# Gates of a product-key expert layer: both parts summed in PSUM and multiplied into G by VectorE

## The chip, the cores and the metric

One core of a Trainium2 chip runs the kernel. The metric is the time of one execution in microseconds (us) on the device; the figure compared is the median of several runs. Engines are named as in the profile: PE is TensorE (PEld its weight loads), DVE is VectorE, ACT is ScalarE, POOL is GpSimd, SP is the queue that issues the transfers.

## The reference, cut to what matters

Two layers; each has a token mixer and then an expert layer (PEER). The expert layer works on 1024 real tokens (and 16 meta tokens in the first layer) with 4096 experts. Per token and head (8 heads), product keys choose 16 experts and a softmax gives each a gate:

```
g = softmax(best_s).reshape(t, 128)                  # 8 heads x 16 gates per token
h_all = einsum('td,nd->tn', xt, u)                   # every expert's hidden value
a = gelu(take_along_axis(h_all, idx)) * g
w = zeros((t, 4096)).at[arange(t)[:, None], idx].add(a)
out = w @ v
```

The kernel computes it densely: G holds, for every expert and token, gelu(hidden) times the sum of the gates that chose this expert (zero for most), and out is G times v.

## The kernel before, in words

The tokens of a layer are worked through in two halves: P (528 tokens in the first layer, with the meta tokens, 512 in the second) and Q (512). An expert's index is m * 32 + r, with m (0 to 127) on the partitions and r a row of 0 to 31, so G is a tile of 128 x 32 x 528 in f32.

- `route` (DVE) finds the 16 experts of each head and token; `slots` turns the result round with PE transposes, so that the 128 choices of a token lie on the partitions: `P.mT` (m of each choice), `P.rT` (its r) and the gate times 2^15 in a high and a low f16 part, `P.gh` and `P.gl`.
- `hidden` loops over the rows r: 24 products (in the first layer's P 48, since its two spans of 272 and 256 tokens are apart) make one row of hidden values in PSUM (L1104), and ACT writes gelu of it into G (L1113). Tokens whose gates are there already take another way: ACT writes gelu into a temporary `ga` (L1110) and POOL multiplies it into G (L1111). In P each piece of weights is split first: ACT rounds it (L273), POOL takes the difference (L280), and SP stores it. In Q the difference is read back instead.
- `gates`, called from `hidden` between rows, does 16 tokens at a time. DVE builds a one-hot matrix `Lh` of m (L1142, 128 x 2048, f16), a one-hot `R[0]` of r (L1144), and the products of `R[0]` with the high part (L1146) and the low part (L1147), each 128 x 512. PE multiplies, for each of the 16 tokens, `Lh` (128 choices x 128 m) by the two parts (128 choices x 32 r).
- In P (L1171) the two parts are 32 products into the same 32 columns of one PSUM bank, so that PSUM adds them. In Q (`P.wide`, L1159) they are 16 products of 64 columns into two banks; ACT copies the high part (L1164) and DVE adds the low part (L1165).
- For the rows that `hidden` has not reached, ACT writes the gates into G (in P L1175), where L1111 meets them later. For the n rows that it has passed, the gates go through ACT (and in Q DVE) into a temporary `gt`, and POOL multiplies them into G: `POOL.tensor_tensor(G[:, 0:n, t0:t0 + 16], gt[:, 0:n], G[:, 0:n, t0:t0 + 16], op=ALU.mult)` (L1177).
- In P the gates are spread over rows 17 to 29 (33 calls in the first layer and 32 in the second, some 2.7 to a row); in Q over rows 6 to 31 (32 calls in each layer, 1.3 to a row). `values` (L1203, L1204, L1209) then multiplies G by v; its first row needs all gates.

`Lh` and `R` have two buffers each, the ring "g" of PSUM has banks 2 and 3 (2 to 5 in Q's gates), and `gt` shares three buffers "ht" with `ga` and with loads. The program is written in the order of the code; a planner, which simulates the engines when the kernel is built, sets the order of instructions on each engine's queue from what it expects to be ready. Each engine then works through its queue in order.

Of the kernel before, what the change touches and what calls it, by code (L numbers as in the profile page):

```python
# [12 lines left out]
F32 = mybir.dt.float32  # L13
# [15 lines left out]
MM = ((3, 0, 2, 0, 0, 3, 0, 0), (3, 0, 2, 0, 0, 3, 0, 0))  # L29
PEND = 29  # L30
QE = 31
WIDE = True
D = 1024
KT = 8
META = 16
# [27 lines left out]
def tile_trunk(ctx, tc, h0, w_pk, wgate, w2, glab, w_out, wqT, keysT, u_pk, v_w, sinks,  # L63
# [30 lines left out]
    for t in ("ah", "al"):  # L94
# [2 lines left out]
    g0 = lay(1, [("wraw", 512, 4), ("ht", 528, 3), ("nsq", 528, 1), ("ndg", 128, 2), ("acc", T, 1), ("nms", 8, 2),  # L97
                 ("nrs", 8, 2), ("rb", 272, 2), ("kt", 128, 2)], 0)
    o = lay(1, [("G", G_EL, 1), ("s", 4096, 1), ("mS", 320, 1), ("rS", 320, 1), ("gS", 640, 1), ("mT", 264, 1), ("rT", 264, 1),
                ("gh", 264, 1), ("glo", 264, 1)], g0)  # L100
    end_p = max(lay(1, [("L", 1024, 2), ("R", 768, 2)], o),
                lay(1, [("X", 1280, 1), ("V", 320, 3), ("I", 320, 3), ("C", 640, 1), ("W", 160, 1), ("J", 160, 1),
                        ("qi", 160, 1), ("rmx", 10, 1), ("rsr", 10, 1)] + [(f"rt{i}", 80, 1) for i in range(8)], o))
    end_p = lay(1, [("iotaM", 256, 1), ("iotaR", 64, 1), ("startT", 80, 1), ("pidxT", 80, 1)], end_p)
# [830 lines left out]
    def peer_setup(qa, qb):  # L935

        P = Layer()
        P.sp = sp = Span(qa.c0, qb.c1)
        P.parts = [(0, qa), (qa.w, qb)]
        P.merge = qa.w == qb.w  # L940
        P.mS = sb([128, 5, 128], F16, "mS")
        P.rS = sb([128, 5, 128], F16, "rS")
        P.gS = sb([128, 5, 128], F32, "gS")
        P.s = [None] * 4
        P.ns = 4 if len(sp.tiles) == 4 else 3
        P.mT = sb([128, 528], F16, "mT")
        P.rT = sb([128, 528], F16, "rT")
        P.gh = sb([128, 528], F16, "gh")
        P.gl = sb([128, 528], F16, "glo")
        P.rows = P.gated = 0  # L950
        P.wide = False
        return P

    def yv(half, lo, k, o, w):
# [163 lines left out]
    def slots(P):  # L1118

        sp = P.sp  # L1120
        for j, (o, m) in enumerate(sp.tiles):
            tp = ps1("g").bitcast(F16)[:, 0:256].rearrange("p (a b) -> p a b", a=2)
            PE.transpose(tp[:, 0, 0:m], P.mS[0:m, j, :], ident16[0:m, 0:m])
            PE.transpose(tp[:, 1, 0:m], P.rS[0:m, j, :], ident16[0:m, 0:m])
            DVE.tensor_copy(P.mT[:, o:o + m], tp[:, 0, 0:m])
            DVE.tensor_copy(P.rT[:, o:o + m], tp[:, 1, 0:m])
            tg = ps1("g")
            PE.transpose(tg[:, 0:m], P.gS[0:m, j, :], ident[0:m, 0:m])
            ACT.activation(P.gh[:, o:o + m], tg[:, 0:m], AF.Copy, scale=GSC)
            DVE.scalar_tensor_tensor(P.gl[:, o:o + m], tg[:, 0:m], GSC, P.gh[:, o:o + m], op0=ALU.mult,  # L1130
                                     op1=ALU.subtract)

    def gates(P, G, iotaM, iotaR):

# [3 lines left out]
        def v4(a, n):  # L1138
# [1 line left out]

        Lh = sb([128, 4, 128, 4], F16, "L", 2)
        DVE.tensor_tensor(Lh, iotaM.unsqueeze(1).to_broadcast([128, 4, 128, 4]), v4(P.mT, 128), op=ALU.is_equal)  # L1142
        R = sb([128, 3, 4, 32, 4], F16, "R", 2)
        DVE.tensor_tensor(R[:, 0], iotaR.unsqueeze(1).to_broadcast([128, 4, 32, 4]), v4(P.rT, 32),  # L1144
                          op=ALU.is_equal)
        DVE.tensor_tensor(R[:, 1], R[:, 0], v4(P.gh, 32), op=ALU.mult)  # L1146
        DVE.tensor_tensor(R[:, 2], R[:, 0], v4(P.gl, 32), op=ALU.mult)  # L1147
        n = P.rows
        gt = sb([128, 32, 16], F32, "ht") if n else None
        outs = [(G[:, n:32, t0:t0 + 16], n, 32)] if n < 32 else []  # L1150
        if n:
            outs.append((gt[:, 0:n], 0, n))
        if P.wide:

            for u in range(2):
                ps = ps1("g")
                for i in range(8 * u, 8 * u + 8):
                    b, t = i // 4, i % 4
                    PE.matmul(ps[:, i % 8 * 64:i % 8 * 64 + 64].rearrange("p (a r) -> p a r", a=2), Lh[:, b, :, t],  # L1159
                              R[:, 1:3, b, :, t], start=True, stop=True)  # L1160
                pv = ps.rearrange("p (t a r) -> p a r t", a=2, r=32)
                for dst, lo, hi in outs:
                    dv = dst[:, :, 8 * u:8 * u + 8]
                    ACT.activation(dv, pv[:, 0, lo:hi], AF.Copy, scale=1.0 / GSC)  # L1164
                    DVE.scalar_tensor_tensor(dv, pv[:, 1, lo:hi], 1.0 / GSC, dv, op0=ALU.mult, op1=ALU.add)  # L1165
        else:
            ps = ps1("g")
            for i in range(16):
                b, t = i // 4, i % 4
                for part in (1, 2):  # L1170
                    PE.matmul(ps[:, i * 32:(i + 1) * 32], Lh[:, b, :, t], R[:, part, b, :, t], start=(part == 1),  # L1171
                              stop=(part == 2))
            pv = ps.rearrange("p (t r) -> p r t", r=32)
            for dst, lo, hi in outs:
                ACT.activation(dst, pv[:, lo:hi], AF.Copy, scale=1.0 / GSC)  # L1175
        if n:
            POOL.tensor_tensor(G[:, 0:n, t0:t0 + 16], gt[:, 0:n], G[:, 0:n, t0:t0 + 16], op=ALU.mult)  # L1177
        P.gated = t0 + 16

    def values(*args, **kw):  # L1180
# [79 lines left out]
    for l in range(DEPTH):  # L1260
# [177 lines left out]
```

## Time and profile before

| | |
|---|---|
| median of 3 runs | 3380.03 us (3378.39 to 3394.43) |
| the profiled execution | 3392.98 us, of which the span 3391.3 us |
| busy share of the span | PE 93%, PEld 78%, DVE 64%, ACT 41%, POOL 32% |
| mean granted TensorE clock | 0.955 of 2.4 GHz |

The span runs from the first to the last instruction of the profiled execution, and times inside it count from its start. That execution is 0.4% above the median of the runs. P's gates lie from about 921 to 1043 us (first layer) and from 2592 to 2724 us (second layer); Q's from about 1365 to 1545 us and from 3010 to 3185 us. A busy share says how long an engine had an instruction in hand, waits for a port included.

### The profile page before, as it was taken

How to read it: one execution, taken by the hardware profiler on the slowest of the kernel's cores; microseconds unless marked ns; L12 is line 12 of the kernel's file. 1: busy time of each engine (PE TensorE's matmuls, PEld its weight loads, DVE VectorE, ACT ScalarE, POOL GpSimd, SP SyncE). 2: the span in 40 equal slices, each digit the busy share in tenths (PEclk: the TensorE clock that was granted, in tenths of full speed). 3: DMA queues.
4: the chain of work that ended last, by engine and by line, in shares of the span. 5: the costliest groups of instructions: out<-in, count | busy, mean ns of one | idle time of the engine just before them, and what ended most of it. 6: DMA issues, size and time to landing. Idle time of an engine off the chain costs nothing.

```text
span 3391.3 us, 64331 instructions
## 1 busy us (share of the span) xinstructions
PE 3157.8 (93%) x22459; PEld 2647.5 (78%) x22459; DVE 2172.3 (64%) x7020; ACT 1381.1 (41%) x3278; POOL 1091.0 (32%) x1092
## 2 busy tenths in 40 slices
PE   7999999989788989999898999999898889999998
PEld 6686887679788988787775868876776678688788
DVE  4645446579896589663326454455698957976547
ACT  4534334433334434444344343344333344344355
POOL 4314022224475232131401231223245643313325
PEclk9899999989889999999997999999898899999999
DMA  8767774564324555445964687755753256554555
GB/s 284 236 202 247 257 245 146 174 217 164 125 88 158 182 178 189 163 152 191 331 232 151 210 274 241 232 170 167 251 173 125 94 179 221 183 189 151 180 173 156
DMA packets 397222, 651.27 MB, mean 192 GB/s; under 512 B 43536, under 2 KB 109152, under 8 KB 396896
## 3 DMA queue, kind: packets, MB, share of 16 engines
q1 hardware_dynamic: 396896, 647.16, 59.3%
q8 instruction: 176, 2.88, 0.4%
q14 instruction: 150, 1.23, 0.1%
HBM read 489.56 MB, written 157.42 MB: 191 GB/s over the span
## 4 chain that ended last, share of the span: by engine, by line
PE 59%; DVE 23%; DMA 6%; ACT 2%; issue 2%; POOL 1%; SPq 0%; POOLq 0%; DVEq 0%; ACTq 0%
PE b L1209 14%; PE b L1104 13%; PE b L334 12%; PE b L980 4%; DVE arena L1142 2%; DMA arena<-h 2%; PE b L704 2%; DVE arena_r L1204 2%; PE b L1159 2%; DVE arena L998 2%; DVE arena L999 2%; PE b L758 1%; DVE arena L1001 1%; PE b L619 1%; DVE arena L1147 1%
## 5 line engine op out<-in xcount | busy, mean ns | idle before, releaser
L280 POOL TENSOR_TENSOR arena_r<-arena,arena_r 128x512 fp32r<-128x512 f32 (+1 forms) x453 | 561.0, 1246 | 867.9 <-ACT arena_r L273 813.9
L1104 PE MATMUL b<-arena_r 128*128 128x512 f32 (+2 forms) x3840 | 782.3, 363 | 23.4 <-ACT arena L1113 13.5
L1209 PE MATMUL b<-arena_r 128*128 128x512 f32 (+2 forms) x4224 | 755.4, 337 | 36.5 <-DVE arena_r L1204 24.7
L1209 PEld LDWEIGHTS b<-arena_r 128*128 128x128 f32 x4224 | 643.8, 190 | 135.8 <-DVE arena_r L1204 41.9
L1104 PEld LDWEIGHTS b<-arena_r 128*128 128x128 f32 x3840 | 643.5, 197 | 123.4 <-ACT arena L1113 14.1
L334 PE MATMUL b<-arena_r 128*128 128x256 f32 (+1 forms) x4992 | 694.6, 293 | 33.8 <-ACT arena_r L273 10.2
L334 PEld LDWEIGHTS b<-arena_r 128*128 128x128 f32 x4992 | 635.1, 193 | 74.4 <-issue 21.8
L273 ACT ACTIVATE arena_r<-arena 128x512 fp32r<-128x512 f32 x456 | 285.1, 629 | 472.4 <-PE b L1104 124.4
L1204 DVE TENSOR_TENSOR arena_r<-arena,arena_r 128x512 fp32r<-128x512 f32 (+2 forms) x352 | 260.5, 751 | 230.9 <-ACT arena_r L1203 230.1
L307 ACT ACTIVATE arena_r<-arena 128x512 fp32r<-128x512 f32 x284 | 178.5, 631 | 327.4 <-PE b L1209 130.5
L980 PE MATMUL b<-arena_r 128*128 128x256 f32 (+1 forms) x1632 | 220.6, 291 | 15.3 <-DMA arena_r<-m_0l 5.3
L1142 DVE TENSOR_TENSOR arena<-arena 128x2048 f16<-128x2048 f16 x129 | 178.8, 1388 | 83.8 <-PE b L1159 83.7
L980 PEld LDWEIGHTS b<-arena_r 128*128 128x128 f32 (+1 forms) x1632 | 205.4, 190 | 27.9 <-DMA arena_r<-m_0l 7.3
L1177 POOL TENSOR_TENSOR arena<-arena 128x448 f32<-128x448 f32 (+20 forms) x129 | 144.2, 1123 | 150.8 <-DVE arena L1165 115.4
L1203 ACT ACTIVATE arena_r<-arena 128x512 fp32r<-128x512 f32 (+2 forms) x352 | 171.7, 502 | 25.2 <-PE b L1209 23.6
L256 POOL TENSOR_TENSOR arena<-arena 128x256 f32<-128x256 f32 (+2 forms) x105 | 90.7, 864 | 271.4 <-ACT arena L255 264.2
L280 DVE TENSOR_TENSOR arena_r<-arena,arena_r 128x256 fp32r<-128x256 f32 (+1 forms) x187 | 101.0, 546 | 92.1 <-ACT arena_r L273 71.2
L716 DVE TENSOR_TENSOR_SCAN arena<-arena,zf 128x384 f32<-128x384 f32 (+6 forms) x116 | 104.3, 903 | 79.0 <-ACT arena L711 77.8
L1111 POOL TENSOR_TENSOR arena<-arena 128x272 f32<-128x272 f32 (+25 forms) x86 | 95.1, 1110 | 158.4 <-DVE arena L1165 141.0
L422 ACT ACTIVATE arena<-b 128x256 f32<-128x256 f32 (+1 forms) x144 | 55.3, 384 | 202.0 <-PE b L334 201.2
L577 POOL TENSOR_TENSOR arena<-arena,mhalf 128x8 f32<-128x8 f32 (+3 forms) x43 | 63.6, 1479 | 210.5 <-DVE arena L574 143.3
L1171 PE MATMUL b<-arena 128*128 128x32 f16 x2080 | 83.5, 192 | 34.2 <-DVE arena L1142 15.9
(273 smaller groups left out, 4240.8 us busy)
## 6 DMA issues: line engine op xcount, KB each, us to landing
arena<-in_v_w_dram SPq DMA_DIRECT2D x288, 256.0 KB, 2.9
arena<-in_u_pk_dram SPq DMA_DIRECT2D x256, 256.0 KB, 3.0
arena_r<-a_0h SPq DMA_DIRECT2D x108, 256.0 KB, 3.7
arena_r<-a_0l SPq DMA_DIRECT2D x108, 256.0 KB, 4.0
arena_r<-a_1h SPq DMA_DIRECT2D x108, 256.0 KB, 3.3
arena_r<-a_1l SPq DMA_DIRECT2D x108, 256.0 KB, 3.9
arena<-m SPq DMA_DIRECT2D x92, 256.0 KB, 4.3
arena<-in_w_pk_dram SPq DMA_DIRECT2D x72, 256.0 KB, 4.3
```

The source lines that it names most:

```text
L273: ACT.activation(hi, src, AF.Copy)
L280: e.tensor_tensor(lo[:, a:b], src[:, a:b], hi[:, a:b].bitcast(F32), op=ALU.subtract)
L307: ACT.activation(hi, wload(src), AF.Copy)
L334: PE.matmul(ps, wt[:, ks], x.at(low, k, xo, sp.w), start=(k == 0 and i == 0), stop=(k == KT - 1 and i == 2))
L716: DVE.tensor_tensor_scan(keep[0:m, 0:wd][:, ::-1], keep[0:m, 0:wd][:, ::-1], zf[0:m, 0:1].to_broadcast([m, wd]), keep[0:m, wd:wd + 1], op0 ...
L980: PE.matmul(ps, yv(half, low, k, oo, m), wt[:, kk * 256:kk * 256 + 256], start=(k == 0 and i == 0 and e == 0), stop=(k == KT - 1 and i == ...
L1104: PE.matmul(ps, wt[:, ks], yv(h, low, k, 0, w // 2 if h is None else w), start=(k == 0 and i == 0), stop=(k == KT - 1 and i == 2))
L1142: DVE.tensor_tensor(Lh, iotaM.unsqueeze(1).to_broadcast([128, 4, 128, 4]), v4(P.mT, 128), op=ALU.is_equal)
L1177: POOL.tensor_tensor(G[:, 0:n, t0:t0 + 16], gt[:, 0:n], G[:, 0:n, t0:t0 + 16], op=ALU.mult)
L1203: ACT.activation(ah, G[:, r, o:o + w], AF.Copy)
L1204: last = DVE.tensor_tensor(al, G[:, r, o:o + w], ah.bitcast(F32), op=ALU.subtract)
L1209: PE.matmul(ps, wt[:, d * 128:d * 128 + 128], pr[low], start=(opens and r == 0 and i == 0), stop=(closes and r == 31 and i == 2))
```

## The change

`gates` has one form for P and Q. The high and low gates lie beside each other in one tile `P.gg`, which `slots` fills; one DVE instruction multiplies `R0` (broadcast over the two parts) by both (128 x 1024). PE always makes 32 products of 32 columns, and PSUM adds the parts. DVE multiplies the n passed rows into G straight from PSUM with one `scalar_tensor_tensor`, in place of ACT's copy into `gt` and POOL's product. ACT still writes the other rows. The four-bank ring of Q's gates goes.

```diff
-        P.gh = sb([128, 528], F16, "gh")
-        P.gl = sb([128, 528], F16, "glo")
+        P.gg = sb([128, 132, 2, 4], F16, "gg")
...
-            ACT.activation(P.gh[:, o:o + m], tg[:, 0:m], AF.Copy, scale=GSC)
-            DVE.scalar_tensor_tensor(P.gl[:, o:o + m], tg[:, 0:m], GSC, P.gh[:, o:o + m], op0=ALU.mult,
-                                     op1=ALU.subtract)
+            g4 = tg[:, 0:m].rearrange("p (b t) -> p b t", t=4)
+            gh, gl = [P.gg[:, o // 4:(o + m) // 4, a] for a in range(2)]
+            ACT.activation(gh, g4, AF.Copy, scale=GSC)
+            DVE.scalar_tensor_tensor(gl, g4, GSC, gh, op0=ALU.mult, op1=ALU.subtract)
...
-        R = sb([128, 3, 4, 32, 4], F16, "R", 2)
-        DVE.tensor_tensor(R[:, 0], iotaR.unsqueeze(1).to_broadcast([128, 4, 32, 4]), v4(P.rT, 32),
-                          op=ALU.is_equal)
-        DVE.tensor_tensor(R[:, 1], R[:, 0], v4(P.gh, 32), op=ALU.mult)
-        DVE.tensor_tensor(R[:, 2], R[:, 0], v4(P.gl, 32), op=ALU.mult)
+        R0 = sb([128, 4, 32, 4], F16, "R0")
+        DVE.tensor_tensor(R0, iotaR.unsqueeze(1).to_broadcast([128, 4, 32, 4]), v4(P.rT, 32), op=ALU.is_equal)
+        R = sb([128, 4, 2, 32, 4], F16, "R")
+        DVE.tensor_tensor(R, R0.unsqueeze(2).to_broadcast([128, 4, 2, 32, 4]),
+                          P.gg[:, t0 // 4:t0 // 4 + 4].unsqueeze(3).to_broadcast([128, 4, 2, 32, 4]), op=ALU.mult)
         n = P.rows
...
+        ps = ps1("g")
+        for i in range(16):
+            b, t = i // 4, i % 4
+            for part in range(2):
+                PE.matmul(ps[:, i * 32:(i + 1) * 32], Lh[:, b, :, t], R[:, b, part, :, t], start=(part == 0),
+                          stop=(part == 1))
+        pv = ps.rearrange("p (t r) -> p r t", r=32)
         if n:
-            POOL.tensor_tensor(G[:, 0:n, t0:t0 + 16], gt[:, 0:n], G[:, 0:n, t0:t0 + 16], op=ALU.mult)
+            gv = G[:, 0:n, t0:t0 + 16]
+            DVE.scalar_tensor_tensor(gv, pv[:, 0:n], 1.0 / GSC, gv, op0=ALU.mult, op1=ALU.mult)
+        if n < 32:
+            ACT.activation(G[:, n:32, t0:t0 + 16], pv[:, n:32], AF.Copy, scale=1.0 / GSC)
...
-        Q.wide = WIDE
...
-        set_rings(g=(2, 3, 4, 5))
         hidden(l, Q, G, HQ, 32, "h", cst, QE)
-        set_rings(g=(2, 3))
```

## Rows read from the trace of the kernel before

**Rows 1.** Stretch, length, busy us (instructions) of PE, PEld, DVE, ACT, POOL; clock, DMA

```profile
921.00:1043.00 122.00, 105.26 (x1503) 102.05 (x1502) 116.70 (x124) 40.48 (x116) 92.00 (x68) 0.88 0.27 88
2592.00:2724.00 132.00, 111.12 (x1301) 91.60 (x1299) 117.49 (x118) 44.19 (x114) 94.79 (x69) 0.86 0.31 102
1365.00:1545.00 180.00, 177.06 (x1130) 144.44 (x1129) 108.37 (x266) 78.61 (x232) 55.43 (x60) 0.98 0.47 149
3010.00:3185.00 175.00, 171.04 (x1113) 140.35 (x1111) 108.14 (x267) 76.76 (x230) 58.19 (x59) 0.99 0.47 150
```

**Rows 2.** Chain of waits by line, 921 to 1043 us, then 2592 to 2724 us

```profile
by line: DVE arena L1142 34.2%; DVE arena L1147 21.3%; DVE arena L1146 13.7%; PE b L1104 9.2%; PE b L1171 7.6%; DVE arena L1144 6.8%; issue 6.3%; ACT arena L1175 0.5%; DVE arena_r L1204 0.4%; DVEq L1146 0.0%
...
by line: PE b L1104 35.1%; DVE arena L1142 20.1%; PE b L1171 13.6%; DVE arena L1147 12.3%; DVE arena L1146 7.5%; issue 5.1%; DVE arena L1144 3.9%; DMA arena<-h 1.5%; POOL arena L1111 1.0%; ACT arena L1175 0.2%
```

**Rows 3.** Groups by line, 921 to 1043 us: count | busy us, mean ns | idle before

```profile
L1142 DVE TENSOR_TENSOR arena<-arena 128x2048 f16<-128x2048 f16 x31 | 48.8, 1574 | 0.0
L1171 PE MATMUL b<-arena 128*128 128x32 f16 x1056 | 43.7, 191 | 16.7 <-DVE arena L1142 7.3 <-DVE arena L1147 5.9 <-DVE arena L1146 2.5
L1177 POOL TENSOR_TENSOR arena<-arena 128x288 f32<-128x288 f32 (+11 forms) x32 | 43.2, 1354 | 15.8 <-ACT arena L1175 15.8
...
L1147 DVE TENSOR_TENSOR arena<-arena 128x512 f16<-128x512 f16 x31 | 30.3, 979 | 0.0
L1146 DVE TENSOR_TENSOR arena<-arena 128x512 f16<-128x512 f16 x31 | 26.2, 846 | 5.8 <-PE b L1171 5.7
...
L1144 DVE TENSOR_TENSOR arena<-arena 128x512 f16<-128x512 f16 x29 | 17.8, 646 | 0.1
```

**Rows 4.** The same groups, 2592 to 2724 us

```profile
L1142 DVE TENSOR_TENSOR arena<-arena 128x2048 f16<-128x2048 f16 x30 | 46.9, 1563 | 0.0
L1177 POOL TENSOR_TENSOR arena<-arena 128x288 f32<-128x288 f32 (+11 forms) x32 | 43.0, 1349 | 18.3 <-ACT arena L1175 15.5 <-PE b L1104 2.3 <-DMA u_0l<-arena_r 0.5
L1171 PE MATMUL b<-arena 128*128 128x32 f16 x1024 | 39.7, 192 | 17.5 <-DVE arena L1142 8.6 <-DVE arena L1147 6.2 <-DVE arena L1146 2.5
...
L1147 DVE TENSOR_TENSOR arena<-arena 128x512 f16<-128x512 f16 x30 | 28.9, 965 | 0.0
L1146 DVE TENSOR_TENSOR arena<-arena 128x512 f16<-128x512 f16 x30 | 27.4, 914 | 12.6 <-PE b L1171 12.5
L1144 DVE TENSOR_TENSOR arena<-arena 128x512 f16<-128x512 f16 x28 | 21.8, 804 | 0.1
```

**Rows 5.** Lines L1142 and L1146 over the span: min/median/max ns

```profile
L1142 DVE TENSOR_TENSOR arena<-arena x129: 1207/1218/2332, 904.7 to 3172.4; 128x2048 f16<-128x2048 f16 x129
...
L1146 DVE TENSOR_TENSOR arena<-arena x129: 409/420/1524, 907.5 to 3173.5; 128x512 f16<-128x512 f16 x129
```

**Rows 6.** L1165 by shape over the span: count | busy us, mean ns

```profile
L1165 DVE SCALAR_TENSOR_TENSOR arena<-b,arena 128x64 f32<-128x64 f32 x12 | 2.3, 214 | 0.3 <-ACT arena L1164 0.3
...
L1165 DVE SCALAR_TENSOR_TENSOR arena<-b,arena 128x248 f32<-128x248 f32 x4 | 1.5, 408 | 0.0
```

**Rows 7.** Timeline, 1455 to 1459 us, POOL then DVE: start, duration

```profile
1455.55 1.69 POOL L1111 TENSOR_TENSOR arena<-arena 128x272 f32<-128x272 f32 x1 [4.58 <-DVE arena L1165]
...
1456.52 0.25 DVE L1165 SCALAR_TENSOR_TENSOR arena<-b,arena 128x96 f32<-128x96 f32 x1
1456.68 0.83 DVE L1146 TENSOR_TENSOR arena<-arena 128x512 f16<-128x512 f16 x1
```

**Rows 8.** Timeline of PE: two gates in Q, then two in P

```profile
1440.90 2.17 PE L1159 MATMUL b<-arena 128*128 128x64 f16 x32
...
2592.56 2.32 PE L1171 MATMUL b<-arena 128*128 128x32 f16 x64
```

**Rows 9.** Chain of waits behind Q's last gate, 1528 to 1540 us: start, us

```profile
1530.62 0.45 ACT arena L1164 x2
...
1531.16 0.85 DVE arena L1165 x3
...
1532.08 2.41 POOL arena L1177 x2
```

More of the change, by code (lines that the diff above doesn't have):

```diff
@@ L31 @@
 QE = 31
-WIDE = True
 D = 1024
@@ L99, in tile_trunk @@
     o = lay(1, [("G", G_EL, 1), ("s", 4096, 1), ("mS", 320, 1), ("rS", 320, 1), ("gS", 640, 1), ("mT", 264, 1), ("rT", 264, 1),
-                ("gh", 264, 1), ("glo", 264, 1)], g0)
-    end_p = max(lay(1, [("L", 1024, 2), ("R", 768, 2)], o),
+                ("gg", 528, 1)], g0)
+    end_p = max(lay(1, [("L", 1024, 2), ("R0", 256, 2), ("R", 512, 2)], o),
                 lay(1, [("X", 1280, 1), ("V", 320, 3), ("I", 320, 3), ("C", 640, 1), ("W", 160, 1), ("J", 160, 1),
@@ L947, in peer_setup @@
         P.rT = sb([128, 528], F16, "rT")
-        P.gh = sb([128, 528], F16, "gh")
-        P.gl = sb([128, 528], F16, "glo")
+        P.gg = sb([128, 132, 2, 4], F16, "gg")
         P.rows = P.gated = 0
-        P.wide = False
         return P
@@ L1142, in gates @@
         DVE.tensor_tensor(Lh, iotaM.unsqueeze(1).to_broadcast([128, 4, 128, 4]), v4(P.mT, 128), op=ALU.is_equal)
-        R = sb([128, 3, 4, 32, 4], F16, "R", 2)
-        DVE.tensor_tensor(R[:, 0], iotaR.unsqueeze(1).to_broadcast([128, 4, 32, 4]), v4(P.rT, 32),
-                          op=ALU.is_equal)
-        DVE.tensor_tensor(R[:, 1], R[:, 0], v4(P.gh, 32), op=ALU.mult)
-        DVE.tensor_tensor(R[:, 2], R[:, 0], v4(P.gl, 32), op=ALU.mult)
-        n = P.rows
-        gt = sb([128, 32, 16], F32, "ht") if n else None
@@ L1150, in gates @@
-        outs = [(G[:, n:32, t0:t0 + 16], n, 32)] if n < 32 else []
-        if n:
[L1152 to L1175, printed above, removed]
@@ L1176, in gates @@
-        if n:
-            POOL.tensor_tensor(G[:, 0:n, t0:t0 + 16], gt[:, 0:n], G[:, 0:n, t0:t0 + 16], op=ALU.mult)
+        R0 = sb([128, 4, 32, 4], F16, "R0")
[3 more added lines that the diff above has]
+                          P.gg[:, t0 // 4:t0 // 4 + 4].unsqueeze(3).to_broadcast([128, 4, 2, 32, 4]), op=ALU.mult)
```

## The prediction

> **What bounds the kernel now.** I read the page first (PE 93% busy: the kernel as a whole is TensorE's), then the four stretches in which gates are made, since the change touches nothing else. [rows 1] show two kinds. In Q, PE is busy 98% of the time at a clock of 0.98 to 0.99, and whatever DVE, ACT or POOL do there is under it. In P, PE is busy 86% and 84% at a clock of 0.88 and 0.86, while DVE is busy 96% and 89% and POOL 75% and 72%. The chain of waits of the same stretches says who sets P's pace [rows 2]: the four DVE lines of `gates` are 76.0% of it in the first layer and 43.8% in the second, where PE has 48.7%. The groups by line then say why [rows 3, 4]: PE's idle time before a gate's products is 16.7 and 17.5 us, most of it ended by DVE; and DVE's instructions are far longer than they need be. The one-hot of m takes 1574 ns on average and 1218 ns as a median of the whole span; the 128x512 ones take 646 to 979 ns and 420 ns [rows 3 to 5].
>
> The excess comes from POOL. In [rows 7] POOL has a product in hand from 1455.55 to 1457.24. L1165, which reads PSUM and one SBUF tile, takes its normal 0.25 us beside it; L1146, which reads two SBUF tiles, takes 0.83 us and ends 0.27 us behind POOL. So in P an f16 product of DVE and a product of POOL take turns. In the first layer the four DVE lines took 123.1 us for 31 + 91 instructions; at the medians they would take 31 x 1.218 + 91 x 0.42 = 76.0, so 47.1 us are excess. In the second it is 125.0 - 73.5 = 51.5 us.
>
> **The change part by part.**
>
> POOL's product L1177 goes: 43.2 of POOL's 92.0 busy us in the first stretch (47%), 43.0 of 94.8 (45%) in the second [rows 1, 3, 4]. What this gives back to DVE no row shows directly. From below it is nothing: POOL's other work (weight differences L280, gelu rows L1111) could fill the same turns. From above it is the undisturbed length of the removed products: 1.2 us for 480 elements [rows 9], so about 0.94 for the mean of 376, x 32 = 30 us per layer. I take POOL's share of the excess, between the two: 47.1 x 0.47 = 22.1 and 51.5 x 0.45 = 23.4 us.
>
> DVE's new product reads PSUM, like L1165. That line goes from 214 ns at 64 elements to 408 at 248 [rows 6], 1.05 ns per element and 0.15 us. P's gates meet 18 to 29 passed rows, 376 elements on average: 0.54 us, x 33 = +17.9 and x 32 = +17.4 us. Since such an instruction doesn't wait for POOL [rows 7], POOL can work beside it: it is some 15% and 14% of the stretches, and I take that share off what is left of the excess, -3.8 us in each.
>
> The two products of R become one of 1024. Between 512 and 2048 elements DVE needs 0.52 ns per element [rows 5], so 0.69 us for two of 0.42: -5.1 and -4.9 us. The doubled broadcast is in no row; at L1165's 1.05 ns per element it would be 1.23 us, 0.39 more than the two instructions, +25 us over 65 gates in place of -10. I take 0.69, because L1142 and L1144, with two broadcast inputs, run at that speed.
>
> DVE's sum in P: -22.1 - 3.8 + 17.9 - 5.1 = -13.1 and -23.4 - 3.8 + 17.4 - 4.9 = -14.7 us. It counts where DVE is the chain: x 0.76 and x 0.438 = -10.0 and -6.4, together -16.4 us. PE gets some of its clock back as its pauses shrink. At full clock its 105.3 and 111.1 busy us would shrink by 12% and 14%, 12.6 and 15.6 us; PE is idle for 16.7 + 20.9 = 37.6 us, of which 16.4 is 44%; and PE is 16.8% and 48.7% of the chain: -0.9 and -3.3, together -4.2 us.
>
> In Q PE's products change from 16 of 64 columns to 32 of 32, with each `Lh` loaded twice. Two gates took 2.17 us in Q's form and 2.32 in P's [rows 8]: 0.15 us for each of 32 pairs, +4.8 us, all on the path. DVE falls from four L1165 to one product, ACT from four copies to at most one: nothing gained, PE covers it. With both banks per gate gone, the ring still holds two gates.
>
> At the end of a half, `values` waits for the last gate. Behind Q's last products came ACT 0.45, DVE 0.85 and POOL 2.41 us, 3.9 us in all from 1530.62 to 1534.49 [rows 9]; now there is one DVE product of 0.65 us per gate. I count 2 of the 3.2 us, for both Q's and the second layer's P; the first layer's P has rows of `hidden` left to cover its end. -6 us; from nothing to -10.
>
> At nothing: ACT's second copy in P (ACT is busy 40.5 of 122 us), the buffer "ht" that `gt` no longer takes, the strided writes of `slots`, and SP's queue, in which no transfer is added or moved.
>
> The sum: -16.4 - 4.2 + 4.8 - 6 = -22 us, from 3393 us of the profiled execution to 3371. Against the median, which is 13 us lower, 3380 - 22 = 3358 us.
>
> **The rivals.**
>
> A greater gain: the turns are what holds P back, and all of them come back. The Trainium skill says so (SBUF — State Buffer, "Who interferes with whom"): a DVE instruction with two SBUF inputs contends with a GpSimd instruction that reads SBUF, the loser is blocked until the other has ended, and one with at most one SBUF input, outside the two-port modes, does not contend. [rows 7] agree with both halves. As a mechanism of this kernel: 30 us given back per layer, DVE at -30 - 2.5 + 17.9 - 5.1 = -20 and -30 - 3 + 17.4 - 4.9 = -20 us, with nothing lost to other waits. That would end PE's 37.6 idle us, and half of the 28 us of clock: -37.6 - 14 + 4.8 - 6 = -53, 3327 us. Against it: POOL's 64 turns per layer sum to more than DVE's excess, so turns already overlap.
>
> Even: the other POOL work takes the freed turns. Relief 0: DVE -7 + 17.9 - 5.1 = +6 in the first layer and +5 in the second, on the path +6.5; with +4.8 and -6 that is +5, 3385 us; with half the relief (11 us per layer) -7, 3373. For it: POOL keeps 49 and 52 busy us [rows 1, 3, 4], in pieces that come when ACT and PE release them.
>
> Slower: DVE's queue is in order, and the new product waits for PE. If the planner puts it right behind its own gate's R, ahead of the next gate's `Lh`, DVE stands still while PE makes the 32 products, about 1.2 us (half of 2.32 in [rows 8]), in every gate that PE takes at once. Queued behind are the next `Lh` and R, and PE waits for these. 18 such gates of 65 undo the gain; 33 make it slower by 0.5%; 40 give 3380 - 22 + 48 = 3406. For it: PE waits for DVE before many gates already, so gates are taken at once, and DVE bounds. Against it: `Lh` has only two buffers, so L1146 waits for PE's products already (5.7 and 12.5 us, [rows 3, 4]), and in Q's old form L1146 ran ahead of other gates' L1165 [rows 7]. The slow broadcast product (+25 - -10 = 35 us, by DVE's shares of the chain +21) would give about 3379 alone and belongs to the even case.
>
> **How the numbers follow.** A difference under 0.5% (17 us) is about what a measurement of this kernel can't tell from no change; the three runs lie 16 us apart. Chances: the forecast 0.40, 3340 to 3368, where some 0.33 lies below 3363 and 0.07 above; the greater gain 0.19, 3322 to 3340; even 0.21, 3366 to 3392; slower 0.20, 3397 and more. So faster 0.52, same 0.28, slower 0.20. The range leaves out the worse half of the slower case and little below: 3322 to 3402 us; the forecast's own range is 3340 to 3368. The planner's order is the largest unknown: an edit here can move instructions of other stages too, which no row prices.
>
> **What would show each step.** In P's stretches: POOL busy falls from 92 and 95 us to about 50; the one-hot of m comes down from 1574 towards 1380 ns; the merged product near 0.69 us undisturbed and the new PSUM product near 0.54, the latter no longer beside POOL than without it; PE's idle time before gates falls from 17 to about 10 us, the granted clock rises above 0.90, and the stretches shorten by 10 us each. In Q: two gates take 2.32 us, and the stretches lengthen by about 2.5 us less the shorter end. Wrong would be: DVE idle in P with the new product released by PE (slower); DVE lines as long as before with L280 and L1111 beside them (even); PE busy above 95% in P (greater gain).

## The result, and the profile after

The changed kernel takes 3346.53 us (median of 4 runs, 3342.11 to 3348.4) against 3381.87 us of the kernel before in the same comparison (4 runs, 3378.39 to 3394.43): a ratio of 0.9887, 95% interval 0.9859 to 0.9915, some 35 to 38 us less. The forecast was 3358 us, range 3322 to 3402: right in direction and in range, with a gain some 60% larger than the 22 us forecast. The profiled execution of the changed kernel took 3347.21 us (span 3345.5).

The four stretches of gates after the change, as windows; columns as in [rows 1]:

```profile
927.00:1039.00 112.00, 106.40 (x1593) 104.65 (x1592) 105.46 (x126) 29.29 (x87) 54.33 (x40) 0.97 0.34 108
2567.00:2683.00 116.00, 101.86 (x1303) 86.17 (x1302) 98.14 (x120) 30.51 (x77) 53.02 (x35) 0.91 0.36 115
1357.00:1522.00 165.00, 165.00 (x1581) 135.96 (x1579) 84.52 (x127) 53.01 (x127) 21.76 (x25) 1.00 0.47 149
2978.00:3143.00 165.00, 165.00 (x1581) 136.22 (x1579) 84.51 (x127) 52.58 (x127) 21.02 (x24) 1.00 0.48 149
```

P's two stretches are 10 and 16 us shorter windows than in [rows 1] (the windows are rounded; exact times stand in the table below). POOL's busy time is down from 92 and 95 to 54 and 53 us, and PE's clock up from 0.88 and 0.86 to 0.97 and 0.91. In Q, PE is busy without a gap. The chain of waits by line, P's first stretch and then the second:

```profile
by line: DVE arena L1140 26.1%; DVE arena L1145 25.2%; PE b L1101 14.3%; DVE arena L1157 10.0%; PE b L1152 9.3%; issue 7.8%; DVE arena L1143 6.6%; DVE arena_r L1186 0.6%; DVEq L1157 0.0%; DVEq L1186 0.0%
...
by line: PE b L1101 51.9%; PE b L1152 21.7%; DVE arena L1140 7.2%; DVE arena L1145 6.8%; DVE arena L1157 5.1%; DVE arena L1143 3.8%; issue 3.5%; ACT arena L1159 0.2%; DVEq L1157 0.0%
```

The first stretch is still DVE's (67.9% for its four lines, 76.0% in [rows 2]); the second has become PE's (73.6%, 48.7% before). The lines are now L1140 (one-hot of m), L1143 (`R0`), L1145 (the merged product), L1152 (PE's gates), L1157 (DVE's product from PSUM) and L1101 (`hidden`). Groups by line, P's first stretch, then the second; count | busy us, mean ns | idle before:

```profile
L1140 DVE TENSOR_TENSOR arena<-arena 128x2048 f16<-128x2048 f16 x31 | 42.6, 1374 | 0.0
L1152 PE MATMUL b<-arena 128*128 128x32 f16 x1056 | 39.8, 190 | 5.6 <-DVE arena L1145 5.5
...
L1145 DVE TENSOR_TENSOR arena<-arena 128x1024 f16<-128x1024 f16 x31 | 34.7, 1118 | 0.0
...
L1143 DVE TENSOR_TENSOR arena<-arena 128x512 f16<-128x512 f16 x29 | 18.1, 660 | 0.0
L1157 DVE SCALAR_TENSOR_TENSOR arena<-b,arena 128x288 f32<-128x288 f32 (+11 forms) x33 | 17.6, 535 | 8.5 <-PE b L1152 8.5
...
L1152 PE MATMUL b<-arena 128*128 128x32 f16 x1024 | 37.9, 191 | 13.3 <-DVE arena L1145 13.3
L1140 DVE TENSOR_TENSOR arena<-arena 128x2048 f16<-128x2048 f16 x30 | 37.8, 1261 | 0.0
...
L1157 DVE SCALAR_TENSOR_TENSOR arena<-b,arena 128x288 f32<-128x288 f32 (+11 forms) x32 | 17.2, 539 | 18.5 <-PE b L1152 18.5
```

Beside [rows 3, 4]: the one-hot of m comes down from 1574 and 1563 to 1374 and 1261 ns, and PE waits 5.6 and 13.3 us before its gates in place of 16.7 and 17.5. DVE's wait for PE has moved from L1146 (5.7 and 12.5 us) to L1157 (8.5 and 18.5 us). The merged product takes 683 ns where nothing disturbs it:

```profile
L1145 DVE TENSOR_TENSOR arena<-arena x129: 675/683/1794, 912.8 to 3126.8; 128x1024 f16<-128x1024 f16 x129
```

That is the view of one line over the span, min/median/max ns.

**Where the time went.** I cut P, from the first product of `hidden` to the first of `values`, at the first and the last product of its gates. "Excess" is what DVE's f16 instructions of P's gates took above their undisturbed medians (1.214 us for 2048 elements, 0.683 for 1024, 0.415 for 512), first and second layer. All in us, from the profiled execution of each kernel:

| kernel | first layer: ahead, gates, behind | second layer | P in sum | excess |
|---|---|---|---|---|
| before | 161.0, 121.8, 18.5 | 140.2, 128.0, 3.9 | 573.4 | 49.8, 54.9 |
| the change | 161.9, 111.2, 7.0 | 141.1, 114.7, 1.5 | 537.4 | 26.6, 20.9 |
| e1 | 159.8, 111.6, 7.7 | 141.9, 115.0, 1.6 | 537.6 | 24.9, 27.6 |
| e2 | 159.9, 118.4, 14.9 | 141.6, 125.1, 3.1 | 563.0 | 49.7, 54.6 |
| e3 | 160.2, 125.9, 7.0 | 140.3, 123.8, 1.5 | 558.7 | 41.8, 43.2 |
| e9 | 160.8, 112.6, 7.0 | 139.2, 114.7, 1.6 | 535.9 | 28.0, 23.3 |
| e10 | 161.4, 116.6, 7.0 | 141.4, 118.2, 1.5 | 546.1 | 32.4, 30.2 |
| e5 | 163.2, 121.3, 17.5 | 140.6, 126.0, 3.9 | 572.5 | 46.6, 54.9 |
| e6 | 162.1, 104.3, 13.2 | 142.5, 104.9, 1.6 | 528.6 | 23.5, 27.4 |

P gives 36.0 us: 23.9 in the stretches of gates (249.8 to 225.9), 13.9 behind them (22.4 to 8.5), 1.8 lost ahead. These are single executions: e4's P, whose code is that of before, took 304.0 and 274.4 us, 578.4 in sum, so a difference of up to 2.7 us in a layer says nothing. Q's stage, cut in the same way, changes by +1.3 us in the first layer (225.0 to 226.2) and by -4.4 in the second (229.4 to 225.0). The two profiled executions differ by 46 us; 16.0 of that lies between Q's first and P's second layer (920.5 to 904.5), which no part of the change touches. The other kernels have 904.6 to 917.3 there, with the ratio of e4 (904.6) at 0.9994, so I don't count it; the profiled execution of before was 11 us above its median. P's 36 us are about what the medians show.

### The profile page after: what moved, and what is told of

Same layout as the page of the kernel before. It is cut to its first block, busy times and chain, and to the rows that moved or that the text cites. A ratio compares the mean times of both kernels' runs of the same rounds, so it can differ in the third digit from the quotient of the medians.

```text
span 3345.5 us, 65752 instructions
## 1 busy us (share of the span) xinstructions
PE 3140.4 (94%) x23483; PEld 2642.3 (79%) x23483; DVE 2107.7 (63%) x6764; ACT 1311.3 (39%) x3021; POOL 938.1 (28%) x963
## 3 DMA queue, kind: packets, MB, share of 16 engines
q14 instruction: 145, 1.19, 0.1%
## 4 chain that ended last, share of the span: by engine, by line
PE 61%; DVE 21%; DMA 6%; ACT 2%; issue 2%; POOL 1%; SPq 0%; DVEq 0%; POOLq 0%; ACTq 0%
PE b L1191 15%; PE b L1101 14%; PE b L333 11%; PE b L977 4%; PE b L1152 3%; PE b L703 2%; DVE arena_r L1186 2%; DMA arena<-h 2%; DVE arena L995 2%; DVE arena L996 2%; PE b L757 1%; DVE arena L998 1%; PE b L618 1%; DVE arena L1140 1%; DVE arena L1145 1%
## 5 line engine op out<-in xcount | busy, mean ns | idle before, releaser
L279 POOL TENSOR_TENSOR arena_r<-arena,arena_r 128x512 fp32r<-128x512 f32 (+1 forms) x453 | 557.6, 1238 | 915.0 <-ACT arena_r L272 843.8
L1101 PE MATMUL b<-arena_r 128*128 128x512 f32 (+2 forms) x3840 | 766.4, 359 | 22.9 <-ACT arena L1110 13.4
L1191 PE MATMUL b<-arena_r 128*128 128x512 f32 (+2 forms) x4224 | 752.5, 337 | 31.9 <-DVE arena_r L1186 22.1
L1101 PEld LDWEIGHTS b<-arena_r 128*128 128x128 f32 x3840 | 630.7, 193 | 123.0 <-ACT arena L1110 14.0
L333 PE MATMUL b<-arena_r 128*128 128x256 f32 (+1 forms) x4992 | 700.9, 294 | 27.5 <-ACT arena_r L272 6.3
L1140 DVE TENSOR_TENSOR arena<-arena 128x2048 f16<-128x2048 f16 x129 | 172.4, 1338 | 59.7 <-PE b L1152 59.7
L1108 POOL TENSOR_TENSOR arena<-arena 128x272 f32<-128x272 f32 (+26 forms) x86 | 90.0, 1051 | 372.5 <-ACT arena L1159 177.5
L1152 PEld LDWEIGHTS <-arena 128*128 128x128 f16 x4128 | 144.9, 118 | 36.9 <-DVE arena L1145 20.8
L1152 PE MATMUL b<-arena 128*128 128x32 f16 x4128 | 154.0, 190 | 18.9 <-DVE arena L1145 18.8
L279 DVE TENSOR_TENSOR arena_r<-arena,arena_r 128x256 fp32r<-128x256 f32 (+1 forms) x187 | 98.0, 528 | 89.7 <-ACT arena_r L272 72.0
L1157 DVE SCALAR_TENSOR_TENSOR arena<-b,arena 128x288 f32<-128x288 f32 (+21 forms) x129 | 63.7, 499 | 111.6 <-PE b L1152 111.6
```

What stands on the lines that cost most here:

```text
L279: e.tensor_tensor(lo[:, a:b], src[:, a:b], hi[:, a:b].bitcast(F32), op=ALU.subtract)
L333: PE.matmul(ps, wt[:, ks], x.at(low, k, xo, sp.w), start=(k == 0 and i == 0), stop=(k == KT - 1 and i == 2))
L1101: PE.matmul(ps, wt[:, ks], yv(h, low, k, 0, w // 2 if h is None else w), start=(k == 0 and i == 0), stop=(k == KT - 1 and i == 2))
L1152: PE.matmul(ps[:, i * 32:(i + 1) * 32], Lh[:, b, :, t], R[:, b, part, :, t], start=(part == 0), stop=(part == 1))
L1191: PE.matmul(ps, wt[:, d * 128:d * 128 + 128], pr[low], start=(opens and r == 0 and i == 0), stop=(closes and r == 31 and i == 2))
```

## The experiments

**e1: the product from PSUM alone.** The kernel before, with the new DVE product in P only (`gt` is made in Q alone); R's two products and Q's wide form stay.

```diff
+            if n:
+                gv = G[:, 0:n, t0:t0 + 16]
+                DVE.scalar_tensor_tensor(gv, pv[:, 0:n], 1.0 / GSC, gv, op0=ALU.mult, op1=ALU.mult)
...
-        if n:
+        if gt is not None:
             POOL.tensor_tensor(G[:, 0:n, t0:t0 + 16], gt[:, 0:n], G[:, 0:n, t0:t0 + 16], op=ALU.mult)
```

> The kernel before, with one part of the change and in P alone: DVE multiplies the passed rows into G straight from PSUM, so that POOL's product and ACT's copy before it go. R is still two products, Q keeps its wide form. P's stage (first product of hidden to first product of values) was 301.3 and 272.1 us before and 280.1 and 257.3 after the whole change. Theory (POOL's product took turns from DVE's f16 products; with it gone PE's pauses and its low clock go): P falls to 283-288 and 259-264 us, Q stays, 0.990 to 0.993 of before. Rival (the merged product of R and the sums in PSUM brought the gain): P stays within 6 us of before, 0.997 to 1.001.

Measured: 3352.17 us (4 runs), ratio 0.9916 (0.9887 to 0.9944), P 537.6 us as with the whole change, less than the 542 to 552 of the theory. This one part carries the gain in P. What the rest adds is within the intervals.

**e2: everything but that.** The change with POOL's product (and ACT's copy ahead of it) put back.

```diff
-            DVE.scalar_tensor_tensor(gv, pv[:, 0:n], 1.0 / GSC, gv, op0=ALU.mult, op1=ALU.mult)
+            gt = sb([128, 32, 16], F32, "ht")
+            ACT.activation(gt[:, 0:n], pv[:, 0:n], AF.Copy, scale=1.0 / GSC)
+            POOL.tensor_tensor(gv, gt[:, 0:n], gv, op=ALU.mult)
```

> The changed kernel, with the product of the passed rows given back to ACT's copy into a temporary and POOL's product, in P and in Q; the merged product of R and 32 products of 32 columns everywhere stay. Theory: P is back near before, 295-301 and 267-272 us, the four or five microseconds saved by the merged R being all that is left; Q as in the changed kernel or 1 to 3 us longer at its end; 0.996 to 1.001 of before. Rival (merged R and PSUM sums carry the gain): P at 280-285 and 257-262 us, 0.988 to 0.991.

Measured: 3380.73 us (10 runs), ratio 0.999 (0.9973 to 1.0006). P is 10.4 us shorter in the profile, the size forecast for DVE's part of the merged R (5.1 + 4.9), but the time can't be told from no change. The excess is that of before, 49.7 and 54.6 us. Groups by line, P's first stretch of gates:

```profile
L1140 DVE TENSOR_TENSOR arena<-arena 128x2048 f16<-128x2048 f16 x30 | 54.2, 1805 | 2.5 <-PE b L1152 2.5
L1159 POOL TENSOR_TENSOR arena<-arena 128x304 f32<-128x304 f32 (+11 forms) x32 | 46.0, 1445 | 15.4 <-ACT arena L1158 15.4
```

Beside a POOL product per gate the one-hot of m takes 1805 ns, not 1374.

**e3: the change, with an idle POOL product.** P's gates get a POOL product of the same shape as the one removed, into a scratch place that nothing reads.

```diff
             DVE.scalar_tensor_tensor(gv, pv[:, 0:n], 1.0 / GSC, gv, op0=ALU.mult, op1=ALU.mult)
+            if P.extra:
+                dum = sb([128, 32, 16], F32, "dum")
+                POOL.tensor_tensor(dum[:, 0:n], gv, gv, op=ALU.mult)
```

> The changed kernel, and in P's gates POOL squares the n passed rows of G that DVE has just written into a scratch tile, in the shape of the product that the change removed; nothing reads the scratch tile, and no buffer is shared for it. Theory (turns at the port): the four-instruction excess of DVE returns, the one-hot of m from 1374 and 1261 ns to over 1500, PE pauses and the clock falls below 0.9, P 298-312 and 270-285 us, 1.000 to 1.008 of before, since DVE now has its PSUM product on top. Rival (the gain came from the shorter chain PE, ACT, POOL and from the temporaries that are free): P stays at 280-284 and 257-261 us, 0.988 to 0.991.

Measured: 3373.06 us (10 runs), ratio 0.9965 (0.9945 to 0.9985): between the theory and its rival. Groups by line, first stretch of gates (in this kernel L1161 is the idle product, L1141 the one-hot of m, L1146 the merged product):

```profile
L1161 POOL TENSOR_TENSOR arena<-arena 128x288 f32<-128x288 f32 (+11 forms) x32 | 52.4, 1639 | 21.2 <-DVE arena L1158 20.8 <-DMA u_0l<-arena_r 0.2
L1141 DVE TENSOR_TENSOR arena<-arena 128x2048 f16<-128x2048 f16 x31 | 44.7, 1441 | 0.0
...
L1146 DVE TENSOR_TENSOR arena<-arena 128x1024 f16<-128x1024 f16 x31 | 39.7, 1281 | 0.0
```

The one-hot of m goes from 1374 to 1441 ns, not to the expected 1500, and the merged product from 1118 to 1281. Windows of the two stretches of gates, columns as in [rows 1]:

```profile
924.00:1050.00 126.00, 111.35 (x1588) 109.18 (x1587) 121.54 (x125) 29.14 (x87) 103.18 (x72) 0.93 0.30 94
2581.00:2705.00 124.00, 102.59 (x1300) 86.77 (x1299) 118.27 (x119) 29.94 (x75) 98.63 (x65) 0.88 0.33 107
```

The stretches of gates are back at 249.7 us in sum, where the kernel before has 249.8, and the excess at 41.8 and 43.2. But behind the gates there are 7.0 and 1.5 us, as in the change. So the gain has two parts, and the idle product gives back only the first. What the second is, PE's timeline shows (start, duration). The kernel before, two pairs of gates and the end of the first layer's P:

```profile
943.24 1.19 PE L1171 MATMUL b<-arena 128*128 128x32 f16 x31 [1.19 <-DVE arena L1147]
944.26 5.72 PE L1104 MATMUL b<-arena_r 128*128 128x256 f32 x26
...
952.32 3.43 PE L1104 MATMUL b<-arena_r 128*128 128x272 f32 x26
...
1042.87 18.76 PE L1104 MATMUL b<-arena_r 128*128 128x272 f32 x144
```

The same of the change:

```profile
941.57 4.14 PE L1101 MATMUL b<-arena_r 128*128 128x272 f32 x32
945.55 2.31 PE L1152 MATMUL b<-arena 128*128 128x32 f16 x64
947.70 4.16 PE L1101 MATMUL b<-arena_r 128*128 128x272 f32 x32
...
1038.18 7.33 PE L1101 MATMUL b<-arena_r 128*128 128x272 f32 x58
```

PE's queue now has 32 products of `hidden` between two pairs of gates where it had 26 (and 2 between a pair's first and second load). 531 of them lie inside the first layer's stretch in place of 446, under work for which DVE sets the pace, and 58 are left behind it in place of 144. That is 86 products at 0.13 us (18.76 us for 144), 11.2 us; measured behind the gates are 11.5 less. e3 has the same order (531; in the first layer's P, PE's 2727 products follow each other by line and shape as in the change, and in e9 too), e1 nearly (526), e2 not (466): it is the product from PSUM that moves it. Why the planner places so was not followed further.

**e9: the same place in POOL's queue, but an instruction that only writes.** In e3's diff the two lines in the `if` become:

```diff
+                dum = sb([128, 1024], F32, "dum")
+                POOL.memset(dum, 0.0)
```

> The change, plus one POOL memset of 1024 elements per gate of P into a scratch place that nothing reads (so added work, nothing left out). POOL's memsets of 256 elements took 312 ns in the trace of the change with the idle product, so about 1.25 us here, some 40 us of POOL per layer, as the idle product had (45). It reads nothing from SBUF. If an f16 product of DVE and a POOL instruction exclude each other only while the POOL instruction reads SBUF (the turns): DVE's excess stays near 26 and 21 us, P's two stretches sum to 535 to 545 us as in the change (537), ratio 0.987 to 0.991. If any busy POOL, or the mere added instruction in the planner's order, gave back the 21 us that the idle product did: P near 559, ratio near 0.9965. The Trainium skill (SBUF — State Buffer, Who interferes with whom) says that the contention is with GpSimd instructions that read SBUF, not with one that only writes it.

Measured: 3354.24 us (6 runs), ratio 0.9897 (0.9877 to 0.9917); P 535.9 us and an excess of 28.0 and 23.3, as in the change. A memset took 0.96 us, not the 1.25 expected, so 31.5 and 30.6 us of POOL in P's two layers; e3's idle products took 53.4 and 51.5. Groups by line, 918 to 1043 us:

```profile
L1141 DVE TENSOR_TENSOR arena<-arena 128x2048 f16<-128x2048 f16 x32 | 43.4, 1356 | 0.0
...
L1146 DVE TENSOR_TENSOR arena<-arena 128x1024 f16<-128x1024 f16 x33 | 36.3, 1099 | 0.0
L1161 POOL MEMSET arena<- 128x1024 f32 x30 | 28.7, 955 | 0.9
```

Timeline of POOL and DVE in the first layer:

```profile
945.13 2.98 POOL L1161 MEMSET arena<- 128x1024 f32 x3
...
945.77 1.21 DVE L1141 TENSOR_TENSOR arena<-arena 128x2048 f16<-128x2048 f16 x1
...
946.91 0.68 DVE L1146 TENSOR_TENSOR arena<-arena 128x1024 f16<-128x1024 f16 x1
...
949.03 0.88 DVE L1146 TENSOR_TENSOR arena<-arena 128x1024 f16<-128x1024 f16 x1
949.32 1.73 POOL L279 TENSOR_TENSOR arena_r<-arena,arena_r 128x512 fp32r<-128x512 f32 x1
949.83 1.84 DVE L1144 TENSOR_TENSOR arena<-arena 128x512 f16<-128x512 f16 x2
```

Under three memsets DVE's one-hot takes 1.21 us and its product 0.68, their undisturbed times. Beside L279, a POOL product that reads, two products of 512 elements take 1.84 us, where 0.83 is normal. The Trainium skill (SBUF — State Buffer, "Who interferes with whom") has it so: a DVE instruction with two SBUF inputs contends with a GpSimd instruction that reads SBUF, not with one that only writes it. Every number of this run agrees. I also sorted DVE's instructions of the gates, over the whole span, by what POOL had in hand for at least 0.05 us beside them. The longest of 512, 1024 and 2048 elements take 0.43, 0.69 and 1.22 us beside nothing (193 instructions), 0.42, 0.69 and 1.22 beside memsets alone (36), and 1.54, 1.80 and 2.35 beside POOL instructions that read (158). All 129 products from PSUM, 25 of them beside POOL instructions that read, stay within 0.01 us of 0.15 us and 1.05 ns per element.

**e10: half of the idle product.** e3 with half of the passed rows.

```diff
-                POOL.tensor_tensor(dum[:, 0:n], gv, gv, op=ALU.mult)
+                h = n // 2
+                POOL.tensor_tensor(dum[:, 0:h], gv[:, 0:h], gv[:, 0:h], op=ALU.mult)
```

> The change, plus an idle POOL product per gate of P over half of the passed rows (some 188 elements on average in place of 376), into a scratch place that nothing reads. If a turn costs DVE what POOL's instruction lasts: half of what the full idle product added (21 us to P's two stretches, 15 and 22 us of excess), so P at 545 to 551 us, ratio 0.991 to 0.994. If a turn costs a fixed time whatever its length: near the full one, 555 to 560, ratio 0.995 to 0.9965. If the order of PE's queue was what the idle product changed, and not the turns: excess near 26 and 21, and P anywhere.

Measured: 3363.73 us (6 runs), ratio 0.9943 (0.9923 to 0.9962), P 546.1 us: in the expected 545 to 551, the ratio just above its 0.991 to 0.994. PE's order is that of the change (531 products, 7.0 us behind). The price goes with the length: the stretches of gates grow by 8.9 us for half a product and by 23.8 for a whole one, the excess by 15.1 and 37.5 us in both layers together. POOL's own time does not: a half product is in hand for 1.28 us and a whole one for 1.61 on average, where 1.2 us were enough for 480 elements [rows 9], so POOL's products wait for their turn too.

**e5: the clock by itself.** The kernel before, with three products of 512 columns into a bank that P's gates don't use, behind each gate's `Lh` in P: PE gets work in its pauses, and DVE and POOL get none.

```diff
+            for _ in range(3):
+                PE.matmul(banks[5], ident16, Lh[:, 0], start=True, stop=True)
```

> The kernel before, and in P's gates three idle products of 128 x 512 (about 0.2 us each at full clock, 42 us in all over 65 gates) into a bank that nothing reads, which need only the gate's Lh, so that PE has work while DVE still makes R. It asks what PE's pauses cost besides themselves. Theory (a pause ahead of a gate's products lowers the clock of the products of hidden behind it, and that costs about as much again): PE busy for other work than the fillers falls by 8 to 16 us in P's two stages (495 us before), the granted clock of the stages rises from 0.91 and 0.89 to 0.93 or more, and P's stages grow by less than 20 us for 42 us of added work. Rival (the clock is low for another reason, or costs nothing, since DVE sets the pace): clock as before, and P's stages grow by 30 us or more, or not at all.

Measured: 3383.27 us (10 runs), ratio 0.9984 (0.9966 to 1.0002). Windows over the whole of P in both layers, this kernel:

```profile
766.00:1068.00 302.00, 274.70 (x2828) 258.76 (x2827) 266.60 (x867) 98.71 (x236) 164.63 (x123) 0.95 0.37 121
2453.00:2724.00 271.00, 242.16 (x1896) 189.22 (x1895) 245.41 (x726) 92.08 (x192) 160.12 (x110) 0.95 0.40 131
```

The kernel before:

```profile
764.00:1065.00 301.00, 262.61 (x2727) 257.38 (x2727) 267.99 (x868) 99.98 (x237) 169.80 (x123) 0.91 0.37 122
2456.00:2728.00 272.00, 232.10 (x1798) 186.33 (x1797) 244.55 (x722) 91.80 (x191) 152.70 (x110) 0.89 0.39 129
```

The filler is 27.5 and 26.2 us of PE work (99 and 96 products), and PE's busy time grows by 12.1 and 10.1: PE's other work falls by 15.4 and 16.1 us, where the theory had 8 to 16 in sum, with the clock, which goes from 0.91 and 0.89 to 0.95 (in the stretches of gates alone from 0.88 and 0.87 to 0.99). So PE's pauses do lower the clock, and filling them restores it. But P takes the same time (572.5 us, 573.4 before). A higher clock and 53.7 us of additional PE work together change nothing in P; what the higher clock would give without that work this run does not show.

**e4: Q alone.** The kernel before with Q's gates in P's form.

```diff
-WIDE = True
+WIDE = False
...
-        set_rings(g=(2, 3, 4, 5))
...
-        set_rings(g=(2, 3))
```

> The kernel before, with Q's gates in P's old form: 32 products of 32 columns summed in PSUM, ACT's copy, POOL's product, two banks in the ring. P is untouched. Q's stage was 221.7 and 229.4 us before (first product of hidden to its last in the first layer, to the first product of values in the second), 219.0 and 224.9 after the whole change. Theory (PE's products cost 0.15 us more for two gates and nothing else bounds Q): 222-225 and 230-233 us, 1.000 to 1.003 of before. Rival (fewer copies and additions behind PE's products free Q): 218-220 and 224-226 us, 0.996 to 0.998.

Measured: 3381.83 us (10 runs), ratio 0.9994 (0.9979 to 1.0009). To the first product of `values`, Q's two stages change by +1.2 and -4.2 us. The 219.0 us that the expectation gives for the changed kernel is misread: from the first to the last product of `hidden`, the first layer's Q takes 222.1 us before and 225.7 in the change and in e4. So the first layer comes out just above the theory (222 to 225), the second (225.1) in the rival's range. The part of the change that lies in Q is worth nothing that can be measured.

e4 keeps ACT's copy and POOL's product and still has the stages of the change (226.2 and 225.1 us against 226.2 and 225.0), and so has e2 (226.1 and 224.8). What the form of Q's gates moves is the order: PE's queue now has 24 products of `hidden` behind the last gate, where it had 5 (in the second layer none). PE's timeline at the end of the first layer's Q, in the kernel before, the change and e4:

```profile
1530.89 1.40 PE L1104 MATMUL b<-arena_r 128*128 128x512 f32 x5
...
1516.49 5.81 PE L1101 MATMUL b<-arena_r 128*128 128x512 f32 x24
...
1534.56 5.81 PE L1104 MATMUL b<-arena_r 128*128 128x512 f32 x24
```

**e6: a third buffer for the one-hots.** The change, with DVE able to work one gate further ahead.

```diff
-    end_p = max(lay(1, [("L", 1024, 2), ("R0", 256, 2), ("R", 512, 2)], o),
+    end_p = max(lay(1, [("L", 1024, 3), ("R0", 256, 3), ("R", 512, 2)], o),
```

> The changed kernel with three buffers for Lh and R0 in place of two. Theory (in the changed kernel DVE is no longer full in P, and stands still where both Lh are taken: 8.5 and 18.5 us ahead of the product from PSUM in P's two stretches): P's stages shorten by 4 to 12 us each, from 280.1 and 257.3, 0.982 to 0.988 of before. Rival (DVE's total work and the order of PE's queue set P): within 3 us of the changed kernel's, 0.987 to 0.991.

What it aims at is the end of the second layer's P in the change, here PE's timeline:

```profile
2656.57 2.31 PE L1152 MATMUL b<-arena 128*128 128x32 f16 x64
2661.91 1.25 PE L1152 MATMUL b<-arena 128*128 128x32 f16 x32 [3.02 <-DVE arena L1145]
2664.94 1.25 PE L1152 MATMUL b<-arena 128*128 128x32 f16 x32 [1.78 <-DVE arena L1145]
...
2680.91 1.25 PE L1152 MATMUL b<-arena 128*128 128x32 f16 x32 [1.02 <-DVE arena L1145]
```

`hidden` has run out, and the last eight gates come alone, 2.7 us apart on average, near the 1.21 + 0.41 + 0.68 + 0.59 = 2.89 us that DVE needs for one. Measured: 3343.69 us (4 runs), ratio 0.9871 (0.985 to 0.9892). The second layer's P is 8.3 us shorter (249.0), as the theory has it; the first layer's is not: the gates take 6.9 us less, and 6.2 us of it come back behind them, by the order again. It is the fastest kernel of the study, though its interval overlaps that of the change.

**e7 and e8: all gates done by an earlier row.** The change with the row by which P's gates are done (29) at 25 and 27.

```diff
-PEND = 29
+PEND = 25
```

> The changed kernel with the gates of P spread over rows 17 to 25 in place of 17 to 29 (PEND 25). In the changed kernel the second layer's P ends with eight gates alone after hidden's last product, at 2.8 us each, where PE waits for DVE. Theory (the tail comes from where the gates stand in the order): fewer gates are left behind hidden, P's second stage falls from 257.3 to 245-252 us, the first by 0 to 5; 0.983 to 0.988 of before. Rival (two buffers and DVE's pace set when gates are ready, whatever the order in the code): no change in P beyond 3 us, 0.987 to 0.991.

> The changed kernel with PEND 27. Theory: between the changed kernel and PEND 25: P's second stage 250-256 us, 0.985 to 0.989 of before. Rival: no change, 0.987 to 0.991.

Measured: e7 3369.67 us (10 runs), ratio 0.9957 (0.9939 to 0.9975), worse than the change; e8 3347.87 us (4 runs), ratio 0.9887 (0.9868 to 0.9907), no better. Against the change, P's first and second layer take +5.5 and +7.4 us in e7, and -5.5 and +6.4 in e8. The second layer's P takes 264.7 and 263.7 us, not the expected 245 to 252 and 250 to 256. Not only the order differs: the earlier a gate is done, the fewer rows DVE multiplies for it and the more POOL does (in e7 8% fewer elements in DVE's products, 22% more in POOL's L1108). Nearly the same work in another order is worth 5 to 7 us either way in a layer, two to three times what e4's P differs from that of before: a size to keep in mind for any forecast of a planned kernel.

## Why the prediction was right, and where its size was off

**Its steps, one by one.** Measured values are those of the first and the second layer.

| step | forecast | measured |
|---|---|---|
| POOL busy in P's stretch | about 50 us | 54.3, 53.0 |
| one-hot of m, mean | 1380 ns | 1374, 1261 |
| merged product, undisturbed | 0.69 us | 0.683 |
| DVE's product from PSUM | 0.54 us | 0.535, 0.539 |
| relief of DVE's f16 products from turns | 25.9 + 27.2 = 53.1 us | 23.2 + 34.0 = 57.2 |
| PE's idle time before gates | about 10 us | 5.6, 13.3 |
| granted clock in the stretch | above 0.90 | 0.97, 0.91 |
| the stretch of gates | -10 us each | -10.6, -13.3 |
| behind the gates | 0, -2 | -11.5, -2.4 |
| Q's two stages in sum, to the first product of `values` | +4.8, -4 at the ends | -3.1 |

In Q a pair of gates takes 2.31 us, in P's old form 2.32 [rows 8]:

```profile
1444.58 2.31 PE L1152 MATMUL b<-arena 128*128 128x32 f16 x64
```

**The mechanism holds.** An f16 product of DVE and a POOL instruction that reads SBUF take turns. e3 puts the reading product back and the stretches of gates return from 225.9 to 249.7 us, e10 half of it and they return to 234.8, e9 puts in one that only writes and they stay (227.3). The new product's own cost, 17.6 and 17.2 us, was forecast to 0.3 us, and it doesn't suffer from POOL (within 0.01 us, in e9).

**The step that was wrong** is the one that costed the first layer's end at nothing: "the first layer's P has rows of `hidden` left to cover its end". They do cover it, but they are not free: 144 products ran there at PE's pace, 18.8 us, and with the product from PSUM 86 of them moved in among the gates, where DVE sets the pace. These 11.5 us are the largest part of what the forecast lacks, 13 us by the medians. (In the profiles the stretches of gates give 3.3 us more than their two terms, 16.4 and 4.2, and Q 3.9 us more than its own; 1.8 us are lost ahead of the gates.) The prediction named the planner's order as its largest unknown and gave it no price; e7 and e8 give a size.

**The end of a half** came out near its term by luck. The 6 us were to come from a shorter chain behind the last gate. That holds for the second layer's P: 3.9 us became 1.5, in e1 1.6, in e2, with POOL's product, 3.1. In Q it does not: e2 and e4 have the long chain and the same stages as the change, to 0.2 us. What Q gains comes with the narrow form of PE's products, which the prediction had at a loss of 4.8 us, and the order that it brings.

**The clock** was a term of 4.2 us, PE's gain by its share of the chain of waits. PE's busy time in P fell by 17.7 us (495.1 to 477.4 in the two layers) with the same products. No run shows time from the clock alone: in e5, where it rose together with PE's work, P's time stayed. My reading, not shown, is that the clock makes room on PE, and that the order fills it. In the second layer, where PE has 73.6% of the chain after the change, some of the 13.3 us may be the clock; no run separates it from the turns there.

**The rivals.** Even, because POOL's other work takes the freed turns: excluded, the excess fell by 57 of 105 us. Slower, because DVE waits for PE behind its own gate: DVE's wait at L1157 is 8.5 and 18.5 us, 0.26 and 0.58 us per gate in place of the 1.2 of that case, and 5.7 and 12.5 of it only moved there from L1146. In the change's second layer the product at 2667.73 us starts before PE's gate at 2667.86, so it belongs to the gate before; the planner did not put it behind its own (DVE's line, then PE's):

```profile
2667.73 0.59 DVE L1157 SCALAR_TENSOR_TENSOR arena<-b,arena 128x432 f32<-128x432 f32 x1
...
2667.86 1.24 PE L1152 MATMUL b<-arena 128*128 128x32 f16 x32 [1.67 <-DVE arena L1145]
```

The greater gain: DVE's relief came close to it, but 47.5 us of excess remain beside L279 and L1108, and PE still waits 18.9 us for gates.

**Open:** why the planner chose the better order, and what of the second layer's gain is clock and what is turns.

## What to carry to other kernels

Where DVE's two-input SBUF products run far over their median, look at what POOL reads at that time: moving POOL's product to DVE, with one operand from PSUM, took 0.54 us of DVE per gate and gave back 0.9 (57.2 us over 65 gates). Before costing the end of a stage at nothing because other work covers it, count that work: it is paid at its own engine's pace there, and is free only under the engine that sets the pace. A filler that costs a suspect resource nothing else (e5), and an idle instruction put in the place of the one removed (e3, e9, e10), tell causes apart that a profile alone mixes.

## What the runs showed of the hardware

- POOL's memsets don't disturb DVE: 31.5 and 30.6 us of them in P's two layers left DVE's excess nearly as it was (28.0 and 23.3 us against 26.6 and 20.9), where 53.4 and 51.5 us of POOL products, their waits included, added 15.2 and 22.3.
- The merged product, with two inputs that are both broadcast, runs at the 0.52 ns per element of the others: 683 ns for 1024, between 415 for 512 and 1214 for 2048.
- PE's clock fell in its pauses. In the kernel before PE stood still for 0.69 and then 1.19 us, with one product between, and the granted clock fell from 2.4 to 1.2 GHz in the second of these pauses. The 26 products of `hidden` behind took 5.72 us; 26 behind a stream without a pause took 3.43 us (timeline of the kernel before, above). The granted clock of the two, as windows of the kernel before (the number ahead of the last two), is 0.54 and 1.00 of 2.4 GHz, so nearly all of the first ran at 1.2 GHz. With fillers in the pauses (e5) the clock in the stretches of gates rose to 0.99, and P's time did not change.

```profile
944.30:949.90 5.60, 5.60 (x32) 5.54 (x29) 5.22 (x9) 1.65 (x6) 1.56 (x1) 0.54 0.21 57
952.40:955.70 3.30, 3.30 (x31) 3.25 (x28) 3.30 (x4) 1.75 (x5) 3.29 (x4) 1.00 0.51 159
```
